# Where layer 0's last norms are written down, which pools stay open for it, and where the queries of layer 1 lie

## The chip, the cores and the metric
One core of a Trainium2 chip. The metric is device time of one execution in microseconds (us); a lower one is better. Engines: PE (TensorE) multiplies matrices, DVE (VectorE) and ACT (ScalarE) work elementwise, POOL (GpSimd) does a few small operations and starts some transfers, SP (SyncE) only starts transfers. PSUM is the memory into which PE writes, SBUF the one from which all engines read.

## The reference, cut to what matters
Two layers over 256 context and 512 latent tokens with 1024 features. Between layer 0's feed-forward (ffn) and layer 1's attention stands this:

```python
x = x + g2 * rmsnorm(f_lat, norm_g[l, 3])            # layer 0's end, latent; the context alike
...
h_lat = rmsnorm(x, norm_g[l, 0]) * (1.0 + sc1) + sh1  # layer 1's start
...
z = h @ w_in                                          # att_w_in: 8 query, 2 key, 2 value heads of 128
return rmsnorm(q, qn_g), rmsnorm(k, kn_g), v          # then grid_rope on q and k of the latent tokens
```

So each token passes two norms over its 1024 features (a sum of squares, a power, a scaling, an addition to x; then the same once more with scale and shift) before its queries, keys and values can be multiplied. Each query and key head is then normalised over its 128 features and rotated.

## The kernel before, in words
Features lie on the 128 partitions, in 8 column tiles (KD), tokens along the free side. A product in full precision is three matmuls per tile of 128 features (mm3, L191 to L197: high x high, high x low, low x high), so one head or output tile over 256 tokens is 24 matmuls of 256 columns. Tokens come in three groups of 256: the context (0 to 256) and two latent ones (GL: 256 to 512, 512 to 768).

**ffn0** (L752) computes layer 0's feed-forward. Its hidden units are split into a high and a low half (tile gs, in the scratch pool ftmp), stored to memory (gd), and loaded again as gated tiles (gload, L794, on POOL's queue, seven tiles in a pool g2; then hh and hl tiles, L813). The output is summed in four passes (outs, L736) into y. In the last pass (L830 on) the groups come in the order 256, 512, 0. After each group's eight output products, that group's norms are put on a list (along): the generator `done` (L1153) loads x (L90, POOL's queue), then runs postnorm (L293) and prenorm (L248) step by step, and stores x for the latent groups (L1159, SP's queue).

Norms are written down in pieces. Each step of a generator yields a planner's cost in us; tick(us) (L315) hands a credit to the list after each product, and steps are written as long as there is credit. finish() (L333) writes down all that is left, finish(key) what is left up to that key. In the last pass each output product ticks 4 x 0.32. Then finish() stands (L837), pools close, and att_proj (L896) begins.

**Norm steps.** sumsq (L233) squares each tile on ACT (L239, L242, tile sq, three buffers, L241) and adds on DVE (L243, ss). rms (L208) multiplies by ones on PE (L214), scales on DVE (L217, rv) and takes the power on POOL (L220, rr). spread (L223) multiplies the factors out over the partitions on PE (L229). postnorm scales y on DVE (L304, u) and adds to x on POOL (L308); prenorm scales x on DVE (L259), shifts on ACT into the high part hh (L266), and takes the rest hl on DVE (L267).

**att_proj** multiplies queries: heads 0 to 3 for group 256, then heads 0 to 3 for group 512, the keys of both groups, heads 4 and 5 over 512 columns, the context's keys, heads 6 and 7. queries (L910) finishes its group's norms, multiplies, ticks, and lets the tail of the query before it go on (advance); it squares its product on ACT (L921, tile sq of the norms' ring) and copies it with a scale to q (L923). A tail (qtail, L926) takes rms of the squares, two factors on DVE (L930), and the rotation (rope, L885): four copies sw<-q on SP's queue, three DVE operations (L892 to L894). Products have four PSUM buffers (mm), small ones three (aux). The framework orders the instructions of each engine from what is written; buffers of a ring are handed out as written.

Pools: y, the scratch and the weights lie on one side of SBUF's stack; nrm1 (sq, u), g2 and x2 (two buffers of x, cb1) on the other. y's pool closes after ffn0, and the pool kv (keys, values, cosines and a Groups object for the queries, L62) takes its place.

Of the kernel before, what the change touches and what calls it, by code (L numbers as in the profile page):

```python
# [8 lines left out]
F32 = mybir.dt.float32  # L9
F32R = mybir.dt.float32r  # L10
# [6 lines left out]
KD = 8  # L17
# [42 lines left out]


class Groups:  # L62


    def __init__(self, pool, groups):
        self.t = {a // 256: [pool.tile([128, 256], F32, name=f"q{a // 256}_{k}") for k in range(KD)] for a, _ in groups}

    def __call__(self, k, a, b):
        return self.t[a // 256][k][:, a % 256:a % 256 + b - a]
# [33 lines left out]
class Trunk:  # L103
# [648 lines left out]
    def ffn0(self, y, h, closed, done, top):  # L752
# [4 lines left out]
        def put(j):  # L757
            def f(a, b, src):
                t = self.tmp.tile([128, 2, 384], F32R, tag="gs", name="gs", bufs=2)
                self.split(t[:, 0, :b - a], t[:, 1, :b - a], src)  # L760
                nc.sync.dma_start(out=gd[j][:, :, a:b], in_=t[:, :, :b - a].bitcast(F32))
            return f

        w3 = self.pool("w3")
        self.w3 = w3.__enter__()
        tmp = self.pool("ftmp")
# [23 lines left out]
        tp.__exit__(None, None, None)  # L790
        self.left = []
        self.np = top.enter_context(self.pool("nrm1", side="right"))
        with self.pool("g2", side="right") as gp:
# [12 lines left out]
            tmp.__exit__(None, None, None)  # L806
            with self.pool("x2", side="right") as xp:
                x = Byg(xp, "x", 2, nc.gpsimd)
                cb = xp.tile([128, 2048], F32, name="cb1")
# [20 lines left out]
                wo = [self.fo(0, 3, n) for n in (0, 4)]  # L830
                h1 = self.htiles()
                for a, b in GL + GS[:1]:
                    for n in range(KD):
                        self.outs(0, 3, g[3], y, n, wo[n // 4], a, b)
                        self.tick(4 * 0.32)
                    self.along((a, 0), done(x, h1, a, b))
                self.finish()  # L837
# [58 lines left out]
    def att_proj(self, h):  # L896
# [11 lines left out]
        self.q = Groups(ap, GL)  # L908
# [158 lines left out]
    def run(self):  # L1067
        tc, nc, a = self.tc, self.nc, self.a
        with self.pool("const") as cp, self.pool("small", 2) as self.sm, self.pool("raw", 4) as self.rawp, \
# [12 lines left out]
            self.kvp.__exit__(None, None, None)  # L1082
            with self.psum(mm=("mm", 4), aux=("aux", 4)):
                self.layer1(mx)
# [14 lines left out]
    def layer0(self):  # L1099
# [36 lines left out]
        with contextlib.ExitStack() as top:  # L1136
# [29 lines left out]
            self.yctx.__exit__(None, None, None)  # L1166
            self.kvp = self.pool("kv")
            self.ap = self.kvp.__enter__()
            self.att_proj(self.h1)
            assert not self.ada_left  # L1170
# [172 lines left out]
```

## Time and profile before
Three runs: median 1634.58 us (1632.60 to 1635.38). The profiled execution took 1633.65 us.

| | |
|---|---|
| profiled execution, us | 1633.65 |
| its span, first to last instruction, us | 1631.9 |
| mean granted clock of PE | 0.980 |
| PE busy, us | 1538.8 (94%) |
| DVE busy, us | 1004.2 (62%) |
| ACT busy, us | 645.5 (40%) |
| POOL busy, us | 123.3 (8%) |

The busy slices of the page (40 equal ones over the span, each digit tenths of it):

```profile
PE   4999999999899999999999993999998999999997
DVE  5466575644889998874466486568937423344345
PEclk9999999999999999999999995999999999999998
```

A digit 9 is 90% or more. The one low digit of PE after the start, with the one low digit of its clock, is the 25th slice, about 979 to 1020 us: the end of layer 0's ffn and the begin of att_proj.

### The profile page before, as it was taken

The page shows a single profiled execution, that of the slowest core. Times are in us where ns is not written, and L with a number is a line of the kernel's source. Part 1 is how long each engine was busy: PE and PEld are TensorE (multiplying, and loading weights), DVE is VectorE, ACT ScalarE, POOL GpSimd, SP SyncE. Part 2 cuts the span into 40 slices and gives each one's busy share as a digit, 9 for nine tenths or more (in the row PEclk, how much of TensorE's full clock was granted, in tenths as well). Part 3 has the DMA queues.
Part 4 walks back from the last instruction along what each step waited for, and adds up shares of the span by engine and source line. Part 5 has one row for each costly group of instructions (what it writes and reads, how often), then busy time and mean ns, then how long its engine had stood idle before and what let it go on. Part 6 is the DMA issues. An engine that isn't in the chain of part 4 may idle for free.

```text
span 1631.9 us, 26584 instructions
## 1 busy us (share of the span) xinstructions
PE 1538.8 (94%) x10656; PEld 1379.3 (85%) x10656; DVE 1004.2 (62%) x1923; ACT 645.5 (40%) x1228; POOL 123.3 (8%) x166
## 2 busy tenths in 40 slices
PE   4999999999899999999999993999998999999997
PEld 2877777789899999999878993999998888888886
DVE  5466575644889998874466486568937423344345
ACT  3334343254655444443211144448845332222222
POOL 0000000001300000002000042210003000000002
PEclk9999999999999999999999995999999999999998
DMA  9142232342426555438986131230032322332211
GB/s 365 54 156 80 88 121 79 123 154 67 155 69 198 182 192 190 161 127 296 320 293 229 56 104 44 86 105 27 1 107 75 103 89 93 103 103 84 97 52 52
DMA packets 75850, 207.25 MB, mean 127 GB/s; under 512 B 7760, under 2 KB 32848, under 8 KB 75600
## 3 DMA queue, kind: packets, MB, share of 16 engines
q1 hardware_dynamic: 70448, 184.92, 34.3%
q0 software_dynamic: 5136, 20.45, 3.5%
q8 instruction: 83, 1.36, 0.3%
q14 instruction: 39, 0.32, 0.1%
q10 hardware_dynamic: 144, 0.20, 0.0%
HBM read 178.28 MB, written 24.64 MB: 124 GB/s over the span
## 4 chain that ended last, share of the span: by engine, by line
PE 57%; DVE 8%; DMA 4%; ACT 2%; POOL 2%; issue 1%; POOLq 0%; DVEq 0%; ACTq 0%; SPq 0%
PE mm L195 18%; PE mm L196 18%; PE mm L197 18%; DVE ss L243 2%; DMA raw<-adat 1%; DMA gd<-gs 1%; DMA raw<-w_fo 1%; PE pp L1033 1%; POOL x L308 1%; PE aux L214 1%; PE aux L229 1%; POOL rr L220 1%; DVE junk L376 1%; PE st L195 0%; PE st L197 0%
## 5 line engine op out<-in xcount | busy, mean ns | idle before, releaser
L195 PE MATMUL mm<-hh,whi 128*128 128x256 f32 (+2 forms) x1292 | 430.5, 335 | 4.4 <-DVE y L744 3.2
L196 PE MATMUL mm<-hl,whi 128*128 128x256 f32 (+2 forms) x1292 | 426.3, 331 | 0.0
L197 PE MATMUL mm<-hh,wlo 128*128 128x256 f32 (+2 forms) x1292 | 425.9, 331 | 0.3 <-DVE wlo L652 0.2
L195 PEld LDWEIGHTS mm<-hh,whi 128*128 128x128 f32 x1292 | 246.9, 192 | 34.0 <-issue 7.7
L197 PEld LDWEIGHTS mm<-hh,wlo 128*128 128x128 f32 x1292 | 246.9, 191 | 18.1 <-DVE wlo L652 0.4
L196 PEld LDWEIGHTS mm<-hl,whi 128*128 128x128 f32 x1292 | 247.3, 192 | 16.7 <-DVE hl L652 0.2
L651 ACT ACTIVATE whi<-raw 128x1024 fp32r<-128x1024 f32 (+2 forms) x145 | 134.1, 945 | 238.3 <-PE mm L196 120.7
L652 DVE TENSOR_TENSOR wlo<-raw,whi 128x1024 fp32r<-128x1024 f32 (+2 forms) x145 | 156.5, 1094 | 59.2 <-ACT whi L651 57.7
L220 POOL TENSOR_TENSOR rr<-rv,mhalf 128x2 f32<-128x2 f32 (+1 forms) x53 | 43.8, 829 | 1128.6 <-DVE rv L217 1128.6
L688 DVE TENSOR_TENSOR sa<-sa,mm 128x256 f32<-128x256 f32 (+2 forms) x38 | 20.7, 546 | 160.3 <-PE mm L197 160.2
L744 DVE TENSOR_TENSOR y<-y,mm 128x256 f32<-128x256 f32 (+1 forms) x104 | 55.9, 542 | 69.2 <-PE mm L197 68.2
L195 PE MATMUL mm<-hh,w3hi 128*128 128x256 f32 (+2 forms) x284 | 93.5, 330 | 2.8 <-ACT w3hi L651 1.4
L197 PE MATMUL mm<-hh,w3lo 128*128 128x256 f32 (+2 forms) x284 | 92.9, 328 | 1.4 <-DVE w3lo L652 1.4
L196 PE MATMUL mm<-hl,w3hi 128*128 128x256 f32 (+2 forms) x284 | 93.1, 329 | 0.0
L651 ACT ACTIVATE w3hi<-raw 128x1024 fp32r<-128x1024 f32 (+2 forms) x51 | 43.2, 875 | 100.4 <-PE mm L196 76.7
L243 DVE TENSOR_TENSOR ss<-ss,sq 128x256 f32<-128x256 f32 x126 | 59.0, 477 | 34.5 <-ACT sq L242 29.0
L376 DVE SCALAR_TENSOR_TENSOR raw<-raw,cb 128x1024 f32<-128x1024 f32 x48 | 58.6, 1222 | 12.5 <-DMA raw<-adat 11.9
L652 DVE TENSOR_TENSOR w3lo<-raw,w3hi 128x1024 fp32r<-128x1024 f32 (+2 forms) x51 | 50.1, 1001 | 16.4 <-ACT w3hi L651 16.4
L195 PEld LDWEIGHTS mm<-hh,w3hi 128*128 128x128 f32 x284 | 54.0, 191 | 6.5 <-ACT q L715 1.7
L197 PEld LDWEIGHTS mm<-hh,w3lo 128*128 128x128 f32 x284 | 53.9, 190 | 4.7 <-DVE w3lo L652 1.6
L196 PEld LDWEIGHTS mm<-hl,w3hi 128*128 128x128 f32 x284 | 54.1, 191 | 3.1
L195 PE MATMUL mm<-g,whi 128*128 128x256 f32 (+1 forms) x176 | 54.5, 310 | 0.0
(294 smaller groups left out, 3351.7 us busy)
## 6 DMA issues: line engine op xcount, KB each, us to landing
raw<-w_fi SPq DMA_DIRECT2D x88, 512.0 KB, 4.3
raw<-ada SPq DMA_DIRECT2D x48, 512.0 KB, 5.3
raw<-adat SPq DMA_DIRECT2D x48, 512.0 KB, 4.5
raw<-w_fo SPq DMA_DIRECT2D x40, 512.0 KB, 4.5
gd<-gs SPq DMA_DIRECT2D x38, 384.0 KB, 2.8
g<-gd POOLq DMA_DIRECT2D x14, 768.0 KB, 12.0
raw<-w_ab SPq DMA_DIRECT2D x20, 512.0 KB, 4.3
x<-x SPq DMA_DIRECT2D x6, 1024.0 KB, 6.8
```

The costliest lines, as they stand in the source:

```text
L195: self.nc.tensor.matmul(out=out, lhsT=wh, rhs=xh, start=first and i == 0, stop=False, **kw)
L196: self.nc.tensor.matmul(out=out, lhsT=wh, rhs=xl, start=False, stop=False, **kw)
L197: self.nc.tensor.matmul(out=out, lhsT=wl, rhs=xh, start=False, stop=i == n - 1, **kw)
L214: nc.tensor.matmul(out=pc[:, 2 * t:2 * t + 2], lhsT=ss[:, t * 128:(t + 1) * 128], rhs=self.ones[:, 0:2], start=True, stop=True)
L220: nc.gpsimd.tensor_tensor(out=r[:, :nt], in0=v[:, :nt], in1=self.mhalf[:, :nt], op=ALU.pow)
L229: nc.tensor.matmul(out=pb[:, t * 128:(t + 1) * 128], lhsT=r[:, t:t + 1].to_broadcast([128, 128]), rhs=self.ident, start=True, stop=True)
L243: nc.vector.tensor_tensor(out=ss[:, :n], in0=ss[:, :n], in1=sq[:, :n], op=ALU.add)
L376: nc.vector.scalar_tensor_tensor(out=junk, in0=raw, scalar=1.0, in1=self.cb[:, i * 1024:i * 1024 + 1024], op0=ALU.mult, op1=ALU.mult, accu ...
L651: self.nc.scalar.activation(out=hi, in_=src, func=AF.Copy)
L652: (eng or self.nc.vector).tensor_tensor(out=lo, in0=src, in1=hi.bitcast(F32), op=ALU.subtract)
L688: nc.vector.tensor_tensor(out=s[:, :n], in0=s[:, :n], in1=p[1][:, :n], op=ALU.mult)
L744: nc.vector.tensor_tensor(out=y(n, a, b), in0=y(n, a, b), in1=pt[:, :b - a], op=ALU.add)
```

## The change
- ffn0's last `finish()` is left out; what the list still holds is written down by the ticks and finish(key) calls of att_proj, and a finish() stands behind att_proj.
- x's pool is opened on the stack that lives through att_proj (`top`), ahead of g2; cb1 gets a pool of its own (cb) on the other side, which closes before the last pass; gs gets a pool of its own, so that the scratch ftmp can close before x's pool opens.
- y's pool stays open until the attention is done; queries are kept in y's tiles (`self.q = y`), which have the same shape of access, and the class Groups goes.

```diff
-class Groups:
...
-                t = self.tmp.tile([128, 2, 384], F32R, tag="gs", name="gs", bufs=2)
+                t = gs.tile([128, 2, 384], F32R, tag="gs", name="gs", bufs=2)
...
         self.w3 = w3.__enter__()
+        gsp = self.pool("gs")
+        gs = gsp.__enter__()
         tmp = self.pool("ftmp")
...
         tp.__exit__(None, None, None)
+        tmp.__exit__(None, None, None)
         self.left = []
         self.np = top.enter_context(self.pool("nrm1", side="right"))
+        x = Byg(top.enter_context(self.pool("x2", side="right")), "x", 2, nc.gpsimd)
         with self.pool("g2", side="right") as gp:
...
-            tmp.__exit__(None, None, None)
-            with self.pool("x2", side="right") as xp:
-                x = Byg(xp, "x", 2, nc.gpsimd)
-                cb = xp.tile([128, 2048], F32, name="cb1")
+            gsp.__exit__(None, None, None)
+            with self.pool("cb") as cp:
+                cb = cp.tile([128, 2048], F32, name="cb1")
...
-                wo = [self.fo(0, 3, n) for n in (0, 4)]
-                h1 = self.htiles()
-                for a, b in GL + GS[:1]:
-                    for n in range(KD):
-                        self.outs(0, 3, g[3], y, n, wo[n // 4], a, b)
-                        self.tick(4 * 0.32)
-                    self.along((a, 0), done(x, h1, a, b))
-                self.finish()
+            wo = [self.fo(0, 3, n) for n in (0, 4)]
+            h1 = self.htiles()
+            for a, b in GL + GS[:1]:
+                for n in range(KD):
+                    self.outs(0, 3, g[3], y, n, wo[n // 4], a, b)
+                    self.tick(4 * 0.32)
+                self.along((a, 0), done(x, h1, a, b))
...
-        self.q = Groups(ap, GL)
...
             self.kvp.__exit__(None, None, None)
+            self.yctx.__exit__(None, None, None)
...
             self.h1 = self.ffn0(y, h, closed, done, top)
-            self.yctx.__exit__(None, None, None)
             self.kvp = self.pool("kv")
             self.ap = self.kvp.__enter__()
+            self.q = y
             self.att_proj(self.h1)
+            self.finish()
```

## Rows read from the trace of the kernel before

**Rows 1.** Windows: stretch, its length, busy us of five engines, clock, DMA share, GB/s.
```profile
964.90:979.00 14.10, 12.66 (x105) 12.26 (x103) 12.94 (x25) 6.45 (x14) 10.02 (x10) 1.00 0.55 186
979.00:1015.80 36.80, 9.41 (x41) 8.60 (x41) 25.62 (x69) 16.64 (x41) 9.47 (x13) 0.55 0.14 44
1015.80:1079.60 63.80, 63.46 (x434) 59.48 (x434) 38.52 (x112) 25.46 (x57) 14.32 (x18) 0.97 0.33 95
```
**Rows 2.** PE in order of time: start, us, line, operation [idle before, releaser].
```profile
981.62 0.58 PE L214 MATMUL aux<-ones,ss 128*128 128x2 f32 x4 [2.81 <-DVE ss L243]
...
1015.80 0.56 PE L195 MATMUL mm<-hh,whi 128*128 128x256 f32 x1
1016.16 0.41 PE L196 MATMUL mm<-hl,whi 128*128 128x256 f32 x1
1016.37 0.41 PE L197 MATMUL mm<-hh,wlo 128*128 128x256 f32 x1
```
**Rows 3.** Waits from 979 to 1015.8: in total us, times, longest.
```profile
PE aux L214 <- DVE ss L243: 19.6, 3, 9.0
```
**Rows 4.** DVE in order of time: column tiles of second and third group.
```profile
985.86 1.27 DVE L267 SCALAR_TENSOR_TENSOR hl<-u,mods,hh 128x256 fp32r<-128x256 f32 x3
...
990.53 0.87 DVE L267 SCALAR_TENSOR_TENSOR hl<-u,mods,hh 128x256 fp32r<-128x256 f32 x2
...
1014.14 0.90 DVE L267 SCALAR_TENSOR_TENSOR hl<-u,mods,hh 128x256 fp32r<-128x256 f32 x2
```
**Rows 5.** ACT in order of time: query squares and copies.
```profile
1003.49 1.44 ACT L921 ACTIVATE sq<-mm 128x256 f32<-128x256 f32 x3
...
1014.41 1.54 ACT L923 ACTIVATE q<-mm,consts 128x256 f32<-128x256 f32 x4
```
**Rows 6.** PE in order of time: the second group's first scale products.
```profile
964.75 0.50 PE L214 MATMUL aux<-ones,ss 128*128 128x2 f32 x4
...
968.75 0.71 PE L229 MATMUL aux<-consts,rr 128*128 128x128 f32 x4 [1.25 <-POOL rr L220]
```
**Rows 7.** PE in order of time: first gated products, a wait.
```profile
769.78 0.28 PE L195 MATMUL mm<-g,w3hi 128*128 128x256 f32 x1
769.90 0.28 PE L196 MATMUL mm<-g,w3hi 128*128 128x256 f32 x1
...
852.09 0.50 PE L195 MATMUL mm<-hh,whi 128*128 128x512 f32 x1 [3.23 <-DVE y L744]
```
**Rows 8.** POOL in order of time: additions to x, powers.
```profile
971.35 7.53 POOL L308 TENSOR_TENSOR x<-x,u 128x256 f32<-128x256 f32 x8
...
996.24 5.87 POOL L308 TENSOR_TENSOR x<-x,u 128x256 f32<-128x256 f32 x8 [1.88 <-DVE u L304]
...
1014.17 1.42 POOL L220 TENSOR_TENSOR rr<-rv,mhalf 128x2 f32<-128x2 f32 x2 [7.47 <-DVE rv L217]
```
**Rows 9.** DVE groups of 1015.8 to 1079.6: busy us, mean ns, idle before.
```profile
L893 DVE TENSOR_TENSOR sw<-sw,sin 128x256 f32<-128x256 f32 x16 | 6.7, 419 | 0.0
...
L930 DVE TENSOR_SCALAR rs<-rr 128x2 f32<-128x2 f32 x21 | 2.5, 165 | 3.1 <-POOL rr L220 2.8
```
**Rows 10.** SP's queue in order of time: the store of x.
```profile
978.91 0.52 SPq L1159 DMA_DIRECT2D xs<-x  x1
```
**Rows 11.** Groups of 979 to 1015.8: the norms' DVE operations.
```profile
L243 DVE TENSOR_TENSOR ss<-ss,sq 128x256 f32<-128x256 f32 x19 | 9.0, 483 | 1.2
...
L267 DVE SCALAR_TENSOR_TENSOR hl<-u,mods,hh 128x256 fp32r<-128x256 f32 x16 | 6.9, 479 | 0.2 <-ACT hh L266 0.2
```
**Rows 12.** POOL in order of time: last gated load, first load of x.
```profile
753.58 0.54 POOL L796 DMA_DIRECT2D g<-gd  x1 [2.95 <-PE mm L197]
...
783.61 0.92 POOL L90 DMA_DIRECT2D x<-x  x1 [1.95 <-DMA hl<-gd]
```
**Rows 13.** Page, part 6: loads, KB each, median us to landing.
```profile
g<-gd POOLq DMA_DIRECT2D x14, 768.0 KB, 12.0
```
**Rows 14.** Window 740 to 770, columns as in Rows 1.
```profile
740.00:770.00 30.00, 30.00 (x174) 30.00 (x173) 12.69 (x19) 10.32 (x17) 7.34 (x14) 1.00 0.95 333
```

More of the change, by code (lines that the diff above doesn't have):

```diff
@@ L59, in __call__ @@
         return self.c[k][:, a:b] if b <= CTX else self.l[k][:, a - CTX:b - CTX]
-class Groups:
[L65 to L69, printed above, removed]
 class Full:
```

## Prediction
> **What bounds the kernel now.** I read the busy shares of the page first: TensorE (PE) is busy for nearly the whole span, with one hole, in the slices about 1000 us. Then the windows around that hole, then PE's timeline inside it, then the waits of the same stretch, then ACT, DVE and POOL in order of time. The reader is to see this. From 964.9 to 979 us PE computes the first four query products (first latent group) at full clock; in the 36.8 us that follow it is busy for 9.41 us, at a mean granted clock of 0.55; then come 63.8 us in which it is busy for 63.46 [rows 1]. In the hole PE does nothing but the norms' small products and waits; the next query product starts at 1015.80 [rows 2]. The largest wait there is for DVE's sums of squares, 19.6 us in three pieces [rows 3]. Other engines are far from full in the hole: DVE 25.62, ACT 16.64 of 36.8 us [rows 1]. It is a chain of dependences, not a full engine.
>
> Two things are late in that chain, and only one of them must be. The next products need the second group's normalised columns; DVE writes the first of those at about 986.3 (the first of three ending after 985.86), the last at 991.4 [rows 4]. They also need a PSUM buffer, and all four of that tag hold the first four products until ACT has squared and copied them: the squares run at 1003.49, the copies from 1014.41 [rows 5]. The products ended at 978.8 (981.62 less the 2.81 of waiting) [rows 2]. ACT had time in between. What held it are the three `sq` buffers: the squares of the queries are written down behind all squares of the norms, which `finish()` has put there, so they get a buffer after the third group's. The order on an engine is not the written one (PE ran four products ahead of norm products written before them), but buffers are handed out in written order.
>
> **The change part by part.** The sum is made against the profiled execution, 1633.65 us (span 1631.9 and 1.75 around it), 0.93 below the median.
>
> *Norms between the queries.* The final `finish()` goes. By the planner's units one group's norm costs 23.6 (0.1, twice 7 x 0.35 + 0.5 + 1.6 + 1.0, 8 x 0.75 and 8 x 0.8); the output products of the second and third group pay 2 x 10.24, so 3.1 of the first group are left, which the first query's `finish((256, 0))` writes. Each query of one group then pays 2.56: the second group's squares of y come ahead of query 0's square, its scale factors behind query 1's product, most of its additions to x behind products 2 and 3, its second half ahead of the first product that needs it. The third group's norm is spread over the next eight products. Now the squares of the queries get their buffers ahead of the second group's second half, the four PSUM buffers come free by about 981, and PE waits for the second group's columns alone. As two heads share a weight slot and four PSUM buffers are free, PE can take four products along as each column tile arrives: 12 matmuls at 0.21 us (1016.16 to 1016.37) [rows 2], 2.5 us a tile against DVE's 0.8 (eight in 6.4). So it is full from the first tile on. The gain before delays is 1015.80 - 986.3 = 29.5 us.
>
> *Delays of the second group's chain*, which now shares engines with three query tails:
> - Its first scale product ran at 964.75, ahead of the queries, and the spread at 968.75 [rows 6]. It is now written behind the product of the second head: two products of 24 matmuls at 0.12 us [rows 7] are 5.8 us. Between 0 (it slips into a gap of PE, as the spread did) and 5.8 I take 2.5.
> - POOL computes one power per tail, 0.71 us (1.42 for two) [rows 8], between the eight additions of x. Three of them are 2.1 us; I take 1.5. The additions took 7.53 us beside a busy DVE and 5.87 beside an idler one [rows 8], so company costs them 1.7 us; the second group already pays that.
> - DVE gets three tails: 0.16 and 2 x 0.165 for the factors and 3 x 0.419 for the rotation [rows 9], 1.75 us each, 5.3 in all; between 0 and 5.3 I take 2.5, as part of the chain is POOL's time.
> - The rotation's four copies a tail go through SP, and the store of the second group's x stands in that queue until 978.91, when POOL has finished [rows 10]. A copy behind the store holds DVE's rotation, and DVE's queue with it: 0 to 3 us (POOL's last addition ends at 978.9, the queries' copies could start some 3 us earlier). I take 0 and keep 3 for the range. The loads of x on POOL's queue stay where the data lets them.
>
> Together 6.5 us (0 to 16): PE resumes at about 992.8 and gains 23.0 us. The clock was at its lower level when PE restarted [rows 1] and will be so again for the first products; that term cancels.
>
> In sentences of their own: the Trainium skill, "SBUF — State Buffer", section "Who interferes with whom", says that a DVE instruction with two SBUF inputs and a GpSimd one that reads SBUF exclude each other for a whole instruction. By it each of the second group's eight additions could now wait for one of the tails' rotations, 8 x 0.419 = 3.4 us more, and the result would be 1616.0. The trace agrees in sign, with less: 1.7 us for eight additions in a stretch where DVE was busy for 92% [rows 1, 8].
>
> *The third group's norm* loses its empty stretch (its last column tile is written at 1015.0 [rows 4]) and moves beside PE's products. On DVE it is 24 operations of 0.48 and 14 additions of 0.483 [rows 11], 18.3 us. The stage after the hole has DVE busy for 38.52 of 63.8 us [rows 1]: with these, and less the three tails done earlier, 51.5, or 81%. What waits for it is the context's key product, some 34 us of PE work behind the restart (eight products of 2.9 us, two heads over 512 columns); alone the chain needed 1015.0 - 991.4 = 24 us. Ten us of slack cover it; if a crowded DVE eats them, the price is up to 10 us. I take 1.
>
> *Queries in y's tiles.* The same copies with the same shape to another address. The other groups' parts of y are read by the norms while they are written; the tile's parts have been written and read side by side before. Nothing.
>
> *Pools in layer 0's feed-forward.* x's 16 KB now lie ahead of the gated tiles, so the last of the seven tiles move over the closing scratch pool, and x's two early loads (1 MB each, first issued at 783.61) can go as soon as their place is free, ahead of gated tiles. The last gated load was issued at 753.58 [rows 12], its kind lands after 12.0 us [rows 13], and the first product that reads such a tile starts at 769.78 [rows 7]: 4.2 us of cover. Later issue by about 2.6 us (the scratch's last additions end near 756.1) and 2 MB ahead of it at 333 GB/s [rows 14], 6 us, make 8.6: less the cover, 4.4 us of waiting at most. On the other side x no longer stands among the later weight loads, and the 3.23 us that PE lost at 852.09 [rows 7] behind a DVE that waited for data may go. Between +4.4 and -3.2 I take 0.
>
> **Sum.** 23.0 - 1.0 = 22 us: 1611.6 in the profiled execution's terms, 1612.6 against the median.
>
> **The rivals.**
> - *The third group becomes the bound.* DVE takes what is ready in its static order, tails ahead of norm; the context's keys come 10 us late. For: 81% on DVE with waits for copies inside; against: PE has two more heads to take ahead. 1612.6 + 10 = 1622.6.
> - *More is gained.* The chain loses nothing in company, and the wait at 852 goes: 29.5 + 3.2 less 5 of the delays taken, 27.7: 1606.9.
> - *The gated loads are late:* 1612.6 + 4.4 = 1617.0.
> - *It doesn't do what it says.* The engines' order is the planner's; if the squares still get their buffers behind the norms, all stays: 1634.6. Against: buffers followed the written order in this trace.
> - *Slower: the clock.* PE now gets its products in pieces between norm steps. In the hole, with 9.41 us of work in 36.8, it was granted 1.2 GHz for most of the time [rows 1], where a matmul takes 0.21 instead of 0.12 us: 2.2 us more for each product of 24. If pieces keep the clock down from the restart to the context's keys (twelve products' worth), that is 26 us against 22 gained: 1634.6 + 4 = 1638.6. It decides from ten products on (10 x 2.2 = 22). Against: on both sides of the hole, with small waits among the products, the granted clock is 1.00 and 0.97 [rows 1]. Beside it: the Trainium skill, "TensorE: Matmul & The Clock Gate", section "HAM oscillation — how this bites in real kernels", says that bursts of products with waits between restart at the lower level each time; the hole agrees (0.55).
>
> **How the numbers follow.** Forecast 0.58, third group 0.17, more gained 0.10, late loads 0.04, nothing 0.05, slower 0.06. Of the forecast's own range, delays of 0 to 16 us and the feed-forward's -3.2 to +4.4 give 1602 to 1627 at the ends. I take 1603 to 1626, which leaves out nothing changed, slower and the tails of the rest. Faster by over 0.2% (3.3 us, about what a measurement of this kernel can tell from no change): 0.89; within it 0.05; slower 0.06.
>
> **What would show it.** Right: squares and copies of the first four queries directly behind their products (by 982), the next product between 987 and 999 of the old time scale, no wait over 2 us before the context's keys, the attention stage as long as before. Wrong: query squares still behind norm squares; a PE wait on the column tiles of the third group; a granted clock near 0.5 in the stage after the restart; PE waiting at the first gated product.

## The result, and the profile after

The changed kernel takes 1622.01 us (median of six, 1618.92 to 1626.39) against 1633.59 for the one before (1628.82 to 1635.64): a ratio over all runs of 0.9938, 95% interval 0.9922 to 0.9954 (the two medians alone give 0.9929). It is 11.6 us faster by the medians, 10.1 by the ratio, where 22 were forecast; the time lies in the range, the gain is about half. Its profiled execution took 1618.92 us (span 1617.2), the shortest of the six.

Executions of one program differ by some us ahead of the place in question: in two profiles of the changed kernel layer 0's last output product ended 962.0 and 967.4 us behind the start, and in the profiles of all runs below it ended between 962.0 and 971.9. So I read one stage only, from the end of that product to the start of the last score product of the attention: 216.2 us before (964.91 to 1181.14), 205.7 and 204.9 after. The gain of 10.5 to 11.3 us is all in it. Totals of different runs hide a difference of some us in the stage behind what varies ahead of it; each stage is read from one profile (the two of the changed kernel are 0.8 apart).

Windows of the changed kernel, columns as in [rows 1]: the query products of the first group, the hole, from the restart to the first score product.
```profile
961.80:976.60 14.80, 14.45 (x117) 13.71 (x116) 10.11 (x24) 6.93 (x17) 3.43 (x5) 1.00 0.64 206
976.60:994.70 18.10, 3.20 (x17) 2.98 (x15) 13.14 (x35) 6.74 (x19) 7.08 (x10) 0.63 0.25 77
994.70:1067.90 73.20, 68.40 (x449) 63.35 (x449) 52.27 (x154) 35.51 (x80) 22.53 (x27) 0.93 0.29 82
```
The hole shrank from 36.8 us to 18.1 [rows 1]. But the stretch behind it, 63.8 us long before and full (63.46), is now 73.2 long, with 4.8 us of waiting and a clock of 0.93. PE in order of time shows both losses: second group's scale products (first half of its norm, second half), the restart, the first matmuls of head 4, the third group's second scale product, the scale product of a tail, the first score product.
```profile
972.52 0.58 PE L204 MATMUL aux<-ones,ss 128*128 128x2 f32 x4 [0.25 <-DVE ss L233]
...
989.80 0.98 PE L204 MATMUL aux<-ones,ss 128*128 128x2 f32 x4 [12.84 <-DVE ss L233]
...
994.71 1.22 PE L185 MATMUL mm<-hh,whi 128*128 128x256 f32 x4 [0.91 <-ACT hh L256]
...
1022.93 0.40 PE L185 MATMUL mm<-hh,whi 128*128 128x512 f32 x1
1027.25 0.98 PE L204 MATMUL aux<-ones,ss 128*128 128x2 f32 x4 [3.92 <-DVE ss L233]
...
1031.65 0.85 PE L204 MATMUL aux<-ones,sq 128*128 128x2 f32 x4
...
1067.89 0.44 PE L185 MATMUL st<-kh,qh 128*128 128x384 f32 x1 [0.47 <-DVE rv L207]
```
The product at 1027.25 stands in PE's queue four matmuls into head 4's product (L185 at 1022.93, 512 columns), all of whose operands are ready. PE waits 3.92 us for it, and its own time of 0.98 (0.50 at the full clock in [rows 6]) shows the lower clock: in windows of 1 us the granted clock is 0.50, that is 1.2 GHz, from 1026 to 1032. At 1031.65 the same form still takes 0.85.

The second group's first scale product came 0.2 us ahead of the end of the last output product before (964.75 against 964.91 [rows 6]) and comes 10.5 behind it now. ACT in order of time shows why: the last two squares of y are written behind query 0's square, which waits for its product.
```profile
970.34 0.39 ACT L912 ACTIVATE sq<-mm 128x256 f32<-128x256 f32 x1 [1.54 <-PE mm L187]
970.62 0.47 ACT L914 ACTIVATE y<-mm,consts 128x256 f32<-128x256 f32 x1
970.97 0.72 ACT L232 ACTIVATE sq<-y 128x256 f32<-128x256 f32 x2
```
DVE and POOL in the hole: rotations, columns (u) and additions to x now alternate.
```profile
978.27 0.43 DVE L884 TENSOR_TENSOR y<-y,cos 128x256 f32<-128x256 f32 x1 [2.00 <-DMA sw<-y]
...
980.21 0.78 DVE L884 TENSOR_TENSOR y<-y,cos 128x256 f32<-128x256 f32 x1
980.91 0.94 DVE L885 TENSOR_TENSOR sw<-sw,sin 128x256 f32<-128x256 f32 x1
...
982.57 0.46 DVE L294 SCALAR_TENSOR_TENSOR u<-y,gcol,aux 128x256 f32<-128x256 f32 x1
...
983.86 0.76 DVE L921 TENSOR_SCALAR rs<-rr 128x2 f32<-128x2 f32 x2 [0.82 <-POOL rr L210]
```
```profile
975.50 1.43 POOL L298 TENSOR_TENSOR x<-x,u 128x256 f32<-128x256 f32 x2 [0.73 <-DVE u L294]
...
979.98 1.58 POOL L298 TENSOR_TENSOR x<-x,u 128x256 f32<-128x256 f32 x2 [1.69 <-DVE u L294]
982.32 0.84 POOL L298 TENSOR_TENSOR x<-x,u 128x256 f32<-128x256 f32 x1 [0.75 <-DVE u L294]
...
985.07 0.84 POOL L298 TENSOR_TENSOR x<-x,u 128x256 f32<-128x256 f32 x1 [0.56 <-DVE u L294]
```
The eight additions take from 975.50 to 985.91, 10.4 us (7.53 before [rows 8]).

A ledger of PE follows from windows of 1 us over the stage: idle is length less busy time, the clock's loss is busy time times one less the granted clock. What is left, PE's work at full clock, is 178.3 us before and 178.9 after, so the two losses are the whole story (over the runs below that do all of the work, that rest lies between 176.6 and 179.1, so the ledger is good to some 2 us): before 31.3 idle and 6.6 clock, after 21.1 and 5.7. Up to the restart 13.5 of idle and 3.1 of clock are gained; behind it 3.3 and 2.2 are lost again.

### The profile page after: what moved, and what is told of

Read it like the earlier page. It is cut to its first block, busy times and chain, and to the rows that moved or that the text cites. A ratio compares the mean times of both kernels' runs of the same rounds, so it can differ in the third digit from the quotient of the medians.

```text
span 1617.2 us, 26585 instructions
## 1 busy us (share of the span) xinstructions
PE 1538.5 (95%) x10656; PEld 1378.1 (85%) x10656; DVE 1001.6 (62%) x1923; ACT 644.2 (40%) x1228; POOL 120.9 (7%) x166
## 4 chain that ended last, share of the span: by engine, by line
PE 58%; DVE 6%; DMA 5%; ACT 2%; POOL 2%; issue 1%; SPq 0%; POOLq 0%; DVEq 0%; ACTq 0%
PE mm L185 18%; PE mm L186 18%; PE mm L187 18%; DMA gd<-gs 2%; DMA raw<-adat 1%; DVE ss L233 1%; PE pp L1024 1%; DMA raw<-w_fo 1%; POOL x L298 1%; PE aux L204 1%; PE st L185 1%; PE aux L219 1%; PE st L187 1%; PE st L186 1%; DVE wlo L642 1%
## 5 line engine op out<-in xcount | busy, mean ns | idle before, releaser
L185 PE MATMUL mm<-hh,whi 128*128 128x256 f32 (+2 forms) x1292 | 428.6, 334 | 5.0 <-DVE y L734 2.9
L185 PEld LDWEIGHTS mm<-hh,whi 128*128 128x128 f32 x1292 | 246.3, 192 | 34.9 <-issue 7.7
L185 PE MATMUL mm<-hh,w3hi 128*128 128x256 f32 (+2 forms) x284 | 93.3, 330 | 2.8 <-ACT w3hi L641 1.4
L642 DVE TENSOR_TENSOR w3lo<-raw,w3hi 128x1024 fp32r<-128x1024 f32 (+2 forms) x51 | 50.1, 1001 | 16.4 <-ACT w3hi L641 16.4
L185 PEld LDWEIGHTS mm<-hh,w3hi 128*128 128x128 f32 x284 | 53.9, 190 | 6.5 <-ACT q L705 1.7
L185 PE MATMUL mm<-g,whi 128*128 128x256 f32 (+1 forms) x176 | 54.5, 310 | 0.0
```

Of the source, the lines that this page charges most:

```text
L185: self.nc.tensor.matmul(out=out, lhsT=wh, rhs=xh, start=first and i == 0, stop=False, **kw)
L642: (eng or self.nc.vector).tensor_tensor(out=lo, in0=src, in1=hi.bitcast(F32), op=ALU.subtract)
```

## The experiments

All in one table: from the end of the last output product to PE's restart (in e6 the first of two) and to the last score product, the two losses of the ledger (us, from the profile of each), the median and the ratio to runs of the kernel before that were made beside that run.

| run | restart | stage | idle | clock | median | ratio |
|---|---|---|---|---|---|---|
| before | 50.9 | 216.2 | 31.3 | 6.6 | 1633.6 | |
| changed | 32.7 | 205.7 | 21.1 | 5.7 | 1622.0 | 0.9938 [0.9922, 0.9954] |
| e0 | 32.6 | 204.9 | 19.9 | 6.3 | 1622.1 | 0.9932 [0.9910, 0.9955] |
| e1 | 39.3 | 210.5 | 25.6 | 6.3 | 1631.7 | 0.9989 [0.9974, 1.0003] |
| e2 | 50.5 | 217.7 | 32.2 | 7.5 | 1636.1 | 1.0013 [0.9996, 1.0030] |
| e6 | 21.9 | 206.8 | 21.5 | 6.7 | 1628.7 | 0.9975 [0.9962, 0.9988] |
| e5 | 29.8 | 205.4 | 18.0 | 10.8 | 1625.8 | 0.9958 [0.9941, 0.9975] |
| e4 | 28.5 | 202.4 | 15.7 | 9.6 | 1623.1 | 0.9929 [0.9909, 0.9950] |
| e9 | 25.6 | 205.2 | 16.4 | 11.9 | 1624.4 | 0.9944 [0.9924, 0.9964] |
| e10 | 25.8 | 200.9 | 16.5 | 6.0 | 1620.3 | 0.9923 [0.9904, 0.9942] |
| e19 | 26.1 | 201.9 | 14.2 | 10.8 | 1620.4 | 0.9926 [0.9908, 0.9943] |
| e17 | 23.0 | 201.9 | 14.3 | 9.1 | 1620.1 | 0.9926 [0.9914, 0.9939] |
| e3 | 32.6 | 207.7 | 20.3 | 8.3 | 1621.9 | 0.9922 [0.9902, 0.9941] |
| e12 | 32.7 | 211.0 | 23.6 | 9.4 | 1627.9 | 0.9971 [0.9958, 0.9984] |
| e14 | 25.4 | 203.1 | 17.8 | 7.3 | 1621.8 | 0.9942 [0.9919, 0.9965] |
| e18 | 23.0 | 201.5 | 12.0 | 12.2 | 1619.0 | 0.9918 [0.9904, 0.9932] |
| e16 | 32.0 | 201.5 | 18.2 | 7.4 | 1617.8 | 0.9911 [0.9897, 0.9925] |
| e21 | 23.0 | 201.8 | 15.5 | 7.2 | 1623.6 | 0.9944 [0.9923, 0.9965] |
| e22 | 23.0 | 200.0 | 14.1 | 8.3 | 1620.1 | 0.9926 [0.9906, 0.9945] |

**What held PE before: e1, e2, e6.** e1 is the changed kernel with

```diff
                 self.along((a, 0), done(x, h1, a, b))
+            self.finish()
```


> The changed kernel with ffn0's last finish() put back: the norms are again written ahead of the queries; the pools stay open and the queries stay in y's tiles. Theory A (buffers of the norms' sq ring in written order held the queries' squares): the squares of the first four queries again get their buffers behind the third group's, PE restarts at about 1015, 1631 to 1637 us. Theory B (the place of the queries' tiles held their copies: kv's pool took the place of a pool that the third group's norm still used): the copies now have a place of their own, PE restarts at about 990, 1608 to 1622 us. Theory C (either alone is enough to hold the PSUM buffers): restart at about 1015, 1631 to 1637 us.

e2 is the kernel before, and e6 is e1, each with
```diff
-                sq = self.np.tile([128, 256], F32, tag="sq", name="sq", bufs=self.sb)
+                sq = ap.tile([128, 256], F32, tag="qsq", name="qsq", bufs=4)
```


> The kernel before with one edit: the squares of the queries and keys' queries get four buffers of their own in kv's pool, in place of the norms' ring of three; finish() and the pools as before. Theory A (ring): squares and copies of the first four queries directly behind their products, by 984, PE restarts at 986 to 991, 1606 to 1618 us. Theory B (place): copies still wait for the third group's norm, PE restarts at about 1015, 1631 to 1637 us. Theory C (either alone is enough): restart at about 1015, 1631 to 1637 us.

> The changed kernel with ffn0's last finish() put back, as in e1, and with four buffers of their own for the squares of the queries. Theory A (ring) and theory C (ring and place each hold): squares and copies run directly behind the first four products, the second group's norm has its engines to itself up to 991, PE restarts at 986 to 991, and the third group's norm is written ahead of all that follows, so that PE waits for its scale products only if they stand in front of ready products: 1606 to 1618 us. Theory B (place alone): the same as e1, within 3 us.

ACT in order of time, in e1, e2 and e6:
```profile
1009.38 0.95 ACT L232 ACTIVATE sq<-x 128x256 f32<-128x256 f32 x2 [0.45 <-DVE ss L233]
1010.38 0.38 ACT L913 ACTIVATE sq<-mm 128x256 f32<-128x256 f32 x1
1010.66 0.47 ACT L915 ACTIVATE y<-mm,consts 128x256 f32<-128x256 f32 x1
```
```profile
1015.19 0.91 ACT L266 ACTIVATE hh<-u,mods 128x256 fp32r<-128x256 f32 x2 [1.06 <-DVE u L259]
1016.00 0.36 ACT L921 ACTIVATE qsq<-mm 128x256 f32<-128x256 f32 x1
1016.27 0.46 ACT L923 ACTIVATE q<-mm,consts 128x256 f32<-128x256 f32 x1
```
```profile
977.41 0.38 ACT L913 ACTIVATE qsq<-mm 128x256 f32<-128x256 f32 x1 [2.58 <-PE mm L187]
```
In e1 the first query's square comes behind the third group's last square, its copy at once, and PE's restart waits for that copy (8.64 us): the ring alone holds it. In e2 square and copy come behind the third group's last column tile (its new ring lies in kv's pool too, as the queries do). Only with both (e6) do they follow their product. So theory C holds: there were two holds, one behind the other, and [rows 5] shows both (squares at 1003.49, copies at 1014.41). That the second is the place of the queries' tiles follows from e2 against e6, which also differ in the other pools; these were not parted. So e1, with the earlier hold alone, restarts 11.6 us sooner than the kernel before and has a stage 5.7 shorter, which its total barely shows. And e6 gains only 4.9 us: its PE restarts at 21.9 and then stands again, as the third group's second scale product lies ahead of ready products:
```profile
1015.42 0.98 PE L204 MATMUL aux<-ones,ss 128*128 128x2 f32 x4 [9.32 <-DVE ss L233]
```

**Why the second group came late: e0, e4, e5, e9, e10, e17, e19.** e0 is the changed kernel again.

> The changed kernel as it is, a second time beside the others, with a profile of its own: the median of its runs stands at 1622, its first profile at 1618.9. Both theories expect 1619 to 1626 and, in the profile, the same two holes of PE: 12 to 14 us ahead of the second group's second scale product, 2 to 8 us ahead of the third group's. If the second profile is some us slower, the place where it differs shows what varies from run to run.

The stage and both waits (12.72 and 3.95 us) repeat. The span is 3.6 us longer: 5.4 more ahead of the stage, 0.8 less in it and 1.0 less behind it.

e4 writes the first half ahead of the queries; e5 is the changed kernel with e2's ring; e9 has that ring with eight buffers and later tails. The edits of e4 (the first three lines) and of e9's tails:
```diff
         w = [self.wslot(self.a["w_at"][1 + i], 2048) for i in range(2)]
+        self.finish((GL[0][0], 0))
+        self.credit = 0.0
+        self.tick(5.2)
...
             self.tick(n / 100)
-            self.advance()
+            if b > GL[0][1] and hd > 0:
+                self.advance()
```


> The changed kernel with the first half of the second group's norm up to its first scale product and spread written ahead of the queries, as the kernel before had it. Theory D1 (the term of 2.5 for the first scale product was too small: it ran 7.8 us later than before, behind two query products and behind a query's square on ACT, and the whole chain with it): that product at about 965 again, PE restarts 4 to 7 us earlier than in the changed kernel (988 to 991), and the total is 2 to 6 us less (1616 to 1620), less than the restart since the third group's norm then holds PE. Theory D2 (the tails of the queries on DVE and POOL are what delays the chain, wherever it starts): the same start, but restart within 2 us of the changed kernel's, 1620 to 1624 us.

> The changed kernel with four buffers of their own for the squares of the queries, tails where they were. It parts the two edits of the run with later tails, in which the hole between the first group's last query product and the restart was 13.1 us and not 18.1. Theory D1 (the ring: the second group's last squares of y stood behind a query's square, and the first scale product with them): that product at its old place ahead of the queries, the hole 13 to 15 us. Theory D2 (the tails on DVE and POOL): the hole 16 to 18 us. The total is 1619 to 1625 by both, as the third group's scale product follows.

> The changed kernel with eight buffers of their own for the squares of the queries, so that their tails can wait, and no tail written before the second product of the second group. Theory D2 (tails on DVE and POOL delay the chain of the second group): the additions to x on POOL take 7 to 8 us instead of 11, PE restarts at 986 to 990, and the four tails then stand beside the third group's norm; total 1614 to 1619 if these hide, 1620 to 1624 if they make the third group's second scale product later by as much. Theory D1 (late first scale product): as that one is written where it was, restart within 2 us of the changed kernel's, 1620 to 1624 us.

e4 has the scale product at its old place (0.2 us ahead of the last output product's end) and restarts 4.2 us sooner (D1). In e5 it is 1.5 behind that end, the restart 2.9 sooner: the ring, which the forecast had as the hold on queries, now held the norm's squares behind a query's. e9 against e5 is the tails: 4.2 us. Both theories are right, each for a part. None of the three gets its earlier restart into the total. In the stage e4 keeps 3.3 of its 4.2 us, e5 and e9 keep 0.3 and 0.5 of 2.9 and 7.1; over the stage the ledger's clock loss is 9.6 us and more in place of 5.7.

e10 is e4 and e9 together, without the tick of 2.56 in `keys`; e17 adds, and e19 adds to e4:
```diff
+                x.eng = nc.sync if s < CTX else nc.gpsimd
                 x.add(s, self.x1)
```


> The three edits together: first half of the second group's norm ahead of the queries, tails of the first four queries later with squares in buffers of their own, and no tick behind the key products, so that the third group's second scale product stands in PE's queue behind head 4's product. Theory P (what is left are scale products standing in PE's queue in front of products that are ready): restart at 986 to 990 as in the kernel before's undelayed chain, no wait over 2 us from there to the context's keys, clock 0.95 or more from 1000 on, total 1606 to 1613. Theory Q (DVE is full after the restart): the wait moves to the context's keys or to the buffers of the key tails, 1616 to 1622.

> The run with all three edits, with the third group's load of x on SP's queue in place of POOL's. Theory L (that load, which waits for the first group's columns, stands on POOL's queue ahead of the second group's first power): the power follows its scale product within 1 us, PE restarts 20 to 22 us behind the last output product in place of 25.8 (32.7 in the changed kernel), the whole stage 195 to 198 in place of 200.9; total 1612 to 1617. Theory M (the chain of the second group is bound by ACT, DVE and POOL's additions, the load only fills a gap): restart and total within 1.5 us of that run (25.8; 1619 to 1622).

> The changed kernel with the first half of the second group's norm ahead of the queries (one of the runs before) and the third group's load of x on SP's queue; tails and squares as in the changed kernel. Theory L: restart 23 to 25 us behind the last output product in place of 28.5, the second wait for the third group stays at 3 to 5 us, stage 198 to 202 in place of 202.4; total 1615 to 1621. Theory M: 28 to 29, 202 to 203, total 1621 to 1625.

e10's stage is 4 to 5 us shorter than the changed kernel's, its total 1.7 to 1.9 in the medians, within the spread of both. Its time is that of theory Q, and the wait moved to a key tail's power on POOL (3.47 us), a place that neither theory named. The mechanism of L fell. In e17 the scale product ends at 968.5, but the power still comes 7 us later, as DVE reaches its operand (rv) only behind the first group's columns and three weight splits:
```profile
968.00 0.50 PE L204 MATMUL aux<-ones,ss 128*128 128x2 f32 x4
```
```profile
971.99 1.22 DVE L642 TENSOR_TENSOR wlo<-raw,whi 128x1024 fp32r<-128x1024 f32 x1
973.13 1.26 DVE L249 SCALAR_TENSOR_TENSOR u<-x,scol,aux 128x256 f32<-128x256 f32 x3
974.30 1.27 DVE L257 SCALAR_TENSOR_TENSOR hl<-u,mods,hh 128x256 fp32r<-128x256 f32 x3
975.49 0.16 DVE L207 TENSOR_SCALAR rv<-aux 128x2 f32<-128x2 f32 x1
```
```profile
975.79 0.70 POOL L210 TENSOR_TENSOR rr<-rv,mhalf 128x2 f32<-128x2 f32 x1 [14.19 <-DVE rv L207]
```
The restart at 23.0 instead of 25.8 is real, but comes with another order (a spread 15 matmuls sooner, a rotation later), not from the load standing ahead of the power: that runs 7.6 us behind the end of the last output product in e17 and 7.9 in e10. The same edit brings 2.4 us in e19 against e4 and in e18 against e14. So it does act, in all three pairs between L and M, and how it leads to the other order was not traced. e19's stage and total lie in L's ranges.

**What takes it back behind the restart: e3, e12, e14, e16, e18, e21, e22.** e3 leaves the tick of 2.56 out of `keys`, e12 ticks 4.27 instead of 2.56 behind the second group's queries.

> The changed kernel without the tick of 2.56 behind each key product, so that the third group's norm gets less credit before head 4's product. Theory P (PE's order: the third group's second scale product stands in PE's queue a few matmuls into head 4's product, whose columns are ready, and holds them for 3.9 us and the clock with them): that scale product is now written behind head 4's, the wait of 3.9 us at 1027 and the window at a clock of 0.78 go, the first score product comes 4 to 8 us sooner, 1613 to 1619 us. Theory Q (DVE is full: norms, tails and splits of weights together): the wait moves to the context's keys or to a PSUM buffer, 1620 to 1625 us.

> The changed kernel with a larger tick (4.27 in place of 2.56) behind the second group's four query products, so that the third group's norm is written sooner among them, and its second scale product lies in PE's queue within the last key product, a product ahead of where it was. Theory W (the third group's chain is as long as its steps, whatever is written when; PE reaches its scale product sooner and waits longer): a wait of 5 to 8 us there in place of 3.9, the stage as long or up to 3 us longer, 1621 to 1626. Theory V (the chain was late since its steps were handed out late): the scale product is ready when PE comes to it, no wait over 1.5 us, no low clock after it, 1613 to 1618.

e3 removes the wait for the scale product as planned, and PE waits 2.80 us for a key tail's spread, whose power stands on POOL among the third group's additions:
```profile
1029.56 1.23 PE L219 MATMUL aux<-consts,rr 128*128 128x128 f32 x4 [2.80 <-POOL rr L210]
```
The total stays as theory Q has it, though the wait is neither at the context's keys nor at a PSUM buffer; the stage is 2.0 us longer. e12 waits 3.2 us for the scale product, then 3.1 at the first score product, and is 6 us slower than the changed kernel: writing steps sooner doesn't make them sooner. That is theory W in its direction; the wait is shorter than W's 5 to 8 us, and the stage (5.3 us longer) and the total lie above its ranges.

e14 is e10 with that tick back and the latent groups' key tails later; e18 is e14 with e17's edit.

> The run with all three edits, with the key tails of the two latent groups also later (squares in the buffers of their own, five buffers for the keys) and the keys' tick back. In that run PE waited 3.5 us for a power of a key tail that stood on POOL behind the third group's additions to x, and its clock fell. Theory P (each of these waits is a small product standing in PE's queue ahead of ready ones; with the key tails and the third group's second scale product behind head 4's product none is left): no wait over 1.5 us from the restart to the context's keys, from the first group's last output product to the last score product 193 to 198 us in place of 200.9 (216.2 before), total 1611 to 1617. Theory Q (DVE has too much to do between the restart and the context's keys, so a wait of 3 to 4 us comes back wherever the order puts it): 200 us or more, 1619 to 1624.

> The run with the key tails later, with the third group's load of x on SP's queue. Theory L: restart 20 to 22 us behind the last output product in place of 25.4, stage 197 to 200 in place of 203.1, total 1613 to 1619; the small waits among heads 4 to 7 stay. Theory M: within 1.5 us of that run (25.4, 203.1; 1620 to 1623).

In e14 no wait over 1.4 us is left between the restart and 1066 us, as theory P has it, but stage (203.1) and total are Q's: the idle time behind the restart, 7.2 us, stands in small pieces. e18's restart (23.0) and stage (201.5) lie between L and M, its total is in L's range.

e18 has the shortest median of the variants that compute everything, 3.0 us below the changed kernel's (intervals 0.9904 to 0.9932 and 0.9922 to 0.9954 overlap). From its restart PE has no wait over 1.7 us, and yet its stage is 201.5: the clock's loss is 12.2. In two places it falls with no wait. Here is the second, in windows of 2 us (columns as in [rows 1]) and as PE in order of time, in e18:
```profile
1026.00:1028.00 2.00, 2.00 (x16) 1.74 (x15) 1.44 (x6) 1.39 (x4) 0.47 (x1) 1.00 0.00 0
1028.00:1030.00 2.00, 2.00 (x15) 1.87 (x13) 0.46 (x4) 0.00 (x0) 1.58 (x3) 0.76 0.03 8
1030.00:1032.00 2.00, 2.00 (x7) 1.61 (x6) 0.16 (x1) 0.00 (x0) 0.02 (x1) 0.50 0.00 0
1032.00:1034.00 2.00, 2.00 (x6) 1.61 (x5) 0.00 (x0) 0.00 (x0) 0.00 (x0) 0.50 0.00 0
```
```profile
1026.25 0.58 PE L204 MATMUL aux<-ones,ss 128*128 128x2 f32 x4
1026.69 1.03 PE L204 MATMUL aux<-ones,qsq 128*128 128x2 f32 x8
...
1028.13 0.95 PE L204 MATMUL aux<-ones,qsq 128*128 128x2 f32 x8
...
1029.43 0.85 PE L204 MATMUL aux<-ones,qsq 128*128 128x2 f32 x4
```
By these windows it fell at about 1029. Ahead of that PE ran 20 products of two columns with two of 512 among them, as the late tails all come at once. The first is like it: 20 products of two columns from 998.96 on, with a few of 256 among them, PE busy throughout, and the clock at 0.50 from 1002 to 1005. But such a group doesn't always bring the fall. 20 and more of these products stand in 4 us in e10 and in e17, PE is busy for all of it in both, and e10 keeps its clock while e17's falls (the same two windows, e10 first):
```profile
1002.00:1004.00 2.00, 2.00 (x20) 2.00 (x19) 0.74 (x6) 1.32 (x2) 1.45 (x2) 1.00 0.11 29
1004.00:1006.00 2.00, 2.00 (x21) 2.00 (x19) 1.41 (x8) 0.66 (x2) 1.24 (x2) 1.00 0.18 47
```
```profile
1002.00:1004.00 2.00, 2.00 (x18) 2.00 (x18) 0.83 (x5) 1.41 (x2) 1.52 (x3) 0.96 0.00 0
1004.00:1006.00 2.00, 2.00 (x12) 2.00 (x11) 1.50 (x5) 0.00 (x0) 1.52 (x2) 0.50 0.13 33
```
e14 keeps it there as e10 does, e9 loses it as e17 does. What decides was not found, so a difference of some us in clock loss between two single profiles need not come from the edit.

e21 and e22 are e18 with tails going on behind the keys too and without the keys' tick; n is three and two steps of tails a product:
```diff
-            self.pend = [g for g in self.pend if next(g, 0) is None]
+            self.pend = [g for g in self.pend[:n] if next(g, 0) is None] + self.pend[n:]
```


> The first half of the second group's norm ahead of the queries, the third group's load of x on SP's queue, squares of queries and keys in eight buffers of their own, no tick behind the keys, and the tails handed out at most three steps a product, from the second product of the second group on. Theory C (tails written together put many small products of two columns side by side, behind which the clock falls even with no wait): the small products stand two to four at a time, the clock's cost from restart to the last score product 3 to 6 us in place of 11.1, stage 193 to 198 us in place of 201.5; total 1611 to 1617. Theory Q (DVE, POOL and ACT have that much to do, and PE's order gives the time back as waits): idle time grows as the clock's cost shrinks, stage 200 to 203, total 1618 to 1622.

> As the run with three steps a product, with two. The tails of the keys then come as late as heads 6 and 7. Theory C: the clock's cost 3 to 6 us, but 2 to 5 us of waiting for the last tails at the first score product; stage 195 to 200, total 1613 to 1619. Theory Q: 201 to 205, total 1619 to 1624.

The clock's loss falls from 12.2 to 7.2 and 8.3, in C's direction (from the restart on 6.1 and 7.1, where C had 3 to 6), and idle time grows from 12.0 to 15.5 and 14.1, as Q has it. e21's stage is Q's and its total above both ranges; e22's stage (200.0) is the upper end of C's, its total Q's. With e14 at 7.3 on the clock without this edit, this theory C is not shown. What sets the floor of some 22 us of loss was not found.

e16 leaves the context group's norms out:
```diff
+                if s < CTX:
+                    for k in range(KD):
+                        self.split(h1[0](k, s, e), h1[1](k, s, e), y(k, s, e))
+                        yield 0.8
+                    return
                 x.add(s, self.x1)
```


> The changed kernel with the context group's norms left out: its columns are taken from y by one copy (ACT) and one subtraction (DVE) a tile, with no load of x, no sums of squares, powers or additions; all else as it is. Theory R (the third group's norm costs the time after the restart: PE's wait of 3.9 us for its scale product, the low clock behind it, DVE's and POOL's time beside the key tails): no wait there, from the restart to the last score product 165 to 168 us in place of 173, from the last output product to the last score product 197 to 200 in place of 205; total 1613 to 1617. Theory S (the tails and weight splits cost it, whoever stands beside them): 171 to 173, total 1620 to 1624.

From the restart to the last score product it takes 169.4 us, between R and S: of the 7.6 us that this stretch grew by (165.3 to 173.0), 3.5 go with the third group's norm. By the ledger, good to some 2 us, these are mostly PE's own work that is no longer there (175.8 us against 178.9 over the stage): idle time and clock loss behind the restart are 9.7 us against 10.2. So the losses there are not the third group's alone. Without it, PE waits 3.19 us for the last query tail at the first score product (1065.27, for DVE's rv), and the clock is 0.50 from 1065 to 1070.

## Why the prediction was right in the mechanism and wrong in the size

**What bounds the kernel** was read rightly as a chain, but its second half named one hold where there were two. "What held it are the three `sq` buffers" explains squares at 1003, not copies at 1014 [rows 5]; that gap of 11 us stood in the rows and was not asked about. With it falls the "Nothing" for "Queries in y's tiles": a kernel with a ring of their own for the squares and the queries in kv's pool gains nothing (e2), so that part was necessary, as far as e2 can tell with the other pools as before.

**The delays of the second group's chain** are the first step that failed: 6.5 us taken, 11.3 measured (29.5 forecast less the 18.2 by which the restart came sooner, 50.9 to 32.7). In the changed kernel's own rows the first addition to x starts 7.0 us later behind the last output product than before (13.5 against 6.4), the eight additions take 2.9 longer, and 1.4 more pass from there to the restart than passed to the first column tile (986.3). Of the terms "the first scale product", 2.5 with 5.8 as upper end, was mis-sized: the product came 10.7 us later, and e4, which undoes that alone, has 4.2 us of it back. The argument looked at PE, where it could slip into a gap; it was ACT's order and the ring that held its operands. The terms for POOL's powers and DVE's tails, 4.0 together, were about right (e5 to e9: 4.2). The SP term, 0, hid a wait of 2.00 us of DVE for a tail's copies, with the second group's columns behind it; no store of x stood ahead of these copies (it was issued at 985.94), so its reason was another than the one feared. What stood in no term is DVE's order ahead of the power. Before, DVE reached the scale product's operand rv 1.95 us behind the end of the last output product:
```profile
966.86 0.15 DVE L217 TENSOR_SCALAR rv<-aux 128x2 f32<-128x2 f32 x1
```
In e4, e5 and e9, whose scale product is at its old place or 1.5 us behind that end, it reaches it 7.3 us behind, after the first group's columns and three weight splits, as in e17's rows above, and the additions still start 4.6 to 5.1 us later than before. In the changed kernel this lies hidden under the late scale product, and no run here removes it.

**The third group's norm** is the second: 1.0 taken, with up to 10 if a crowded DVE eats the slack; behind the restart 7.6 us were lost (9.4 up to the first score product, of which 1.7 come back in the attention). By the ledger about 3.3 are idle, 2.2 clock, and 2.2 PE's own small products that moved behind the restart. The slack was counted up to the context's key product. What came first was the third group's second scale product in PE's queue, 44 matmuls (the rest of head 4 and head 5) ahead of those keys. That this one wait is the cause is not shown: e3 takes it away and its stage is no shorter, and e16, without that norm, has 3.5 of the 7.6 back. The sum with measured terms: 29.5 - 11.3 - 7.6 = 10.6, the stage's 10.5.

**The rivals.** "The third group becomes the bound", 1622.6, has the measured time by coincidence; its place was wrong, as no product waited for the context's columns, and 4.8 of the 11.4 us that were missing (11.3 less 6.5, and 7.6 less 1.0) lie ahead of the restart. Of the clock rival's 26 us, 2.2 are there: a second fall at 1027 us. Of the clock "that term cancels" held for the restart and not for what follows. That the time lies in the forecast's range is in part luck: the range was worked out from the delays and the feed-forward, and the third group's 7.6 us were not in it.

**Right:** the queries' squares run behind their products (970.34 on), the restart lies 32.7 us behind the last output product (997.6 on the old scale, in the window of 987 to 999), the pools of the feed-forward change nothing that shows (the wait at 852 is 2.87 and 3.61 us in the two profiles, 3.23 before [rows 7]), and the rest of the program takes what it took: 450.8 us behind the last score product before, 449.5 after. Of the signs named, "no wait over 2 us before the context's keys" failed (3.92), and the sign of being wrong "a granted clock near 0.5 in the stage after the restart" came, for some 6 us.

## What to carry to other kernels

When a step is spread among products to fill a hole, look in every in-order queue at what each of its small instructions stands ahead of: a scale product in front of ready matmuls, or a norm's square behind a query's, passes its wait on to all that stands behind it. Then measure what removing it gives: here another wait came up in its place (e3). Keep a ledger of idle time plus clock loss over the stage; here sixteen variants moved the restart by up to 29 us, and no stage was shorter than 200.0. And before blaming one hold, ask whether each later row has the same cause.

## What the runs showed of the hardware

The granted clock fell to 1.2 GHz with no wait of PE ahead of it, while PE was busy by the profile for 2.00 of each 2.00 us, behind 20 products of two columns (e18, 1026 to 1029 us). It was 0.50 from 1030 to 1034. Behind a like group it fell in e9 and e17 and stayed at 1.00 in e10 and e14. The prediction had counted only waits.

Rotations on DVE, with two inputs from SBUF, took 0.78 and 0.94 us beside POOL's additions and 0.42 to 0.43 alone, and POOL's addition 0.84 beside and 0.72 alone; u, with one input from PSUM, took 0.46 beside an addition (982.57). The Trainium skill, "SBUF — State Buffer", section "Who interferes with whom", says that DVE with two SBUF inputs contends with a GpSimd instruction that reads SBUF, and that DVE with at most one does not, outside its two-port modes: the rotations and u agree with both halves. A third row doesn't fall under them: the two factors rs, each with one SBUF input, took 0.76 us beside an addition (983.86) and 0.24 without one (974.80).
